# Windowed attention with split values and scaled probabilities, a mask written through DRAM, and gate columns split earlier

## The chip, the cores and the metric

The kernel runs on one core of a Trainium2 chip. The metric is device time in microseconds (us), the median of several runs of the whole program. A core has a matrix engine (PE, with its weight loads shown as PEld), a vector engine (DVE), a scalar engine (ACT), a general engine (POOL) and a queue engine (SP). Each takes its instructions in the order in which they were written for it; DMA queues move data between DRAM and the on-chip memory, and matmul results land in eight banks of accumulator memory (PSUM), of which this kernel uses four for the large products and four for everything else.

## The reference

One decoder block over 512 tokens of width 2048: a modulated RMS norm, one wide input projection, a gated delta-rule branch and a windowed-attention branch, each projected back and merged by gates. The change touches the attention and the two gate columns per head of the delta rule (`b_a`, `a_a`).

```python
beta = jax.nn.sigmoid(b_a.astype(jnp.float32))
g = -jnp.exp(a_log[l]...) * jax.nn.softplus(a_a... + dt_bias[l]...)
...
qb = rms_norm(q_b.reshape(B, T, SWA_HEADS, SWA_HEAD_DIM), q_norm_gain[l])
kb = rms_norm(k_b.reshape(B, T, SWA_KV_HEADS, SWA_HEAD_DIM), k_norm_gain[l])
vb = v_b.reshape(B, T, SWA_KV_HEADS, SWA_HEAD_DIM)
o_b = sliding_window_attention(qb, kb, vb, sinks[l], rel_bias)
y_swa = (o_b * jax.nn.silu(z_b)) @ w_branch_swa[l]

def sliding_window_attention(q, k, v, sinks, rel_bias):
    # 16 query heads of 64, 4 key heads, blocks of 128 queries that see their own and the previous block
    logits = jnp.einsum("bnqhgd,bnkhd->bnhgqk", qb, kb) * (d ** -0.5)
    logits = jnp.where(valid, logits + bias, -jnp.inf)
    m = jnp.maximum(jnp.max(logits, axis=-1, keepdims=True), sink)
    p = jnp.exp(logits - m)
    probs = p / (jnp.sum(p, axis=-1, keepdims=True) + jnp.exp(sink - m))
    out = jnp.einsum("bnhgqk,bnkhd->bnqhgd", probs, vb)
```

## The kernel before

**The frame.** All large products run as three matmuls on split operands: a float32 number is written as `hi` (rounded by a cast on ACT, L184) plus `lo` (the rest, a subtraction on DVE, L185), and hi·hi, hi·lo and lo·hi are added up. The weights are cut into 464 *halves*. `run` (L236) goes through them: for half s it issues the loads of coming weights on SP, the split of half s+2 (`w_cast`, `whi` on ACT and `wlo` on DVE), then one step of each *lane* (a generator that does other work up to its next `yield`), and then the 12 matmuls of half s. One such round is a *tick*; the order is fixed when the program is written, and every engine keeps it. So the matmuls of the next half stand behind whatever the lanes gave PE in that tick, and `whi`/`wlo` of half s+2 stand behind what the lanes gave ACT and DVE in the tick before. Three weight buffers (`wraw`) of two halves each and four buffers each for `whi` and `wlo` are the slack.

**The lanes.** `gdn_all` (L1380) runs the gates of the delta rule (`gdn_gates`), its two groups of four heads (`gdn_group`), then `swa_bias`, then waits for the attention's inputs and runs `swa_attend` and `load_branches`. `keys_lane` runs `swa_keys`. The small results of the lanes lie in four PSUM banks (`side`, L80) that are taken in turn.

**Gate columns.** `gdn_gates` splits 16 columns of the input projection (`wab` into `wabr`) in the first tick after the first stage (`plan_start`, 8 column blocks in five parts, where DVE also does the convolutions) and multiplies them with all of `hhi` and `hlo` in the following four ticks (`ps_ab`).

**Mask.** `swa_bias` builds 16 rows of 384 values (`vec`) and one POOL DMA writes each of them 128 times to DRAM (`vecd`), from where `load` reads a skewed 128x256 mask per head.

**Attention.** `swa_keys` scales the keys, writes hi and lo twice side by side (`kd`) and transposes them on PE (32 transposes) into `kTh`/`kTl`. `Attn` treats four query heads (a group g, four groups) over four blocks n: `prep` scales the queries and splits them (`qhl`), `turn_q` transposes them (16 transposes per group); `logits` makes 8 matmuls and adds the mask (L1055); `soft` takes exponentials on ACT; `turn` transposes the probabilities (`pT`, one bank per key block); `values` multiplies them in full float32 with the values (each such matmul runs as two passes, 64 columns wide) and divides by the sum; `finish` transposes the result back (8 per group) and multiplies with the gate. `swa_attend` runs block i's `logits`, block i-1's `soft`, block i-2's `turn` and block i-3's `values` in an *iteration* of two ticks, and puts the next group's `norm`, `prep`, `load`, `turn_q` between (`todo`).

Of the kernel before, what the change touches and what calls it, by code (L numbers as in the profile page):

```python
# [16 lines left out]
P = 128  # L17
# [20 lines left out]
def tile_hybrid_block(  # L38
# [539 lines left out]
    def gdn_gates():  # L578
# [10 lines left out]
        yield  # L589
# [46 lines left out]
        V.tensor_copy(t1, gh[:, 0:32].bitcast(F32))  # L636
        yield
# [305 lines left out]
    kTh, kTl = [], []  # L943
# [22 lines left out]
    def swa_keys():  # L966
        rsqrt(flat(rs_[:, 16:20]), flat(sq[:, 16:20]), 16, 1.0 / HD, EPS)
        kd_ = [s4("kd", F32R).rearrange("p (t h w d) -> p t h w d", t=2, h=4, w=2) for _ in range(2)]

        def turn_keys(kT_):  # L970
            for h in range(4):
                pt = side("ps_kT")
                for t in range(NT):
                    TE.transpose(pt[:, t * P:(t + 1) * P],
                                 kd_[t // 2][:, t % 2, h].rearrange("p w d -> p (w d)").bitcast(F32), ident)
                if h % 2 == 0:
                    kT_.append(v3(s4("kT", F32R), 2))
                S.copy(kT_[h // 2][:, h % 2], pt)
                if h % 2 == 1:
                    yield  # L980
# [11 lines left out]
        yield from turn_keys(kTh)  # L992
        for t in range(NT):
            for w in range(2):
                kw = kd_[t // 2][:, t % 2, :, w]
                V.tensor_tensor(kw, k3(t), kw.bitcast(F32), op=ALU.subtract)
            yield
        yield
        yield from turn_keys(kTl)
# [3 lines left out]
    class Attn:  # L1003
# [25 lines left out]
        def turn_q(self, i):  # L1029
            if i == 0:  # L1030
                self.qT = []
            self.qT.append(v3(s4("qT", F32R), 2))
            for h in (2 * i, 2 * i + 1):
                pt = side("ps_qT")
                for t in range(NT):
                    TE.transpose(pt[:, t * P:(t + 1) * P],
                                 self.qhl[t // 2][:, t % 2, h].rearrange("p w d -> p (w d)").bitcast(F32), ident)
                S.copy(self.qT[i][:, h % 2], pt)
# [44 lines left out]
        def values(self, n, pT, mx):  # L1083
            g = self.g
            V.tensor_tensor(mx[:, 3], mx[:, 3], mx[:, 4], op=ALU.add)
            V.reciprocal(mx[:, 3], mx[:, 3])
            V.tensor_scalar(mx[:, 3], mx[:, 3], 0.5, None, op0=ALU.mult)
            if n == 0:
                self.osb = s4("osb").rearrange("p (t n) -> p t n", t=NT)
            pv = side("ps_pv")  # L1090
            for h in range(4):
                for kb in pT:
                    t = n - 1 + kb
# [366 lines left out]
```

## Time and profile before

| | |
|---|---|
| median of 3 runs | 1537.3 us (1535.39 to 1538.13) |
| the profiled execution | 1534.27 us, its span 1532.5 us |
| busy: PE, DVE, ACT, POOL | 97%, 54%, 36%, 4% of the span |
| mean granted clock of PE | 0.989 |
| the chain that ended last | PE 89%, DVE 5%, DMA 4% |

How to read it: the span goes from the first to the last instruction. A matmul's listed time is that of one through the pipeline, so consecutive ones overlap; the distance of their starts is what one costs. In a list of groups, "idle before" is time in which the engine waited ahead of that group, with what ended the wait. In a timeline, a wait stands in brackets behind the row. [...]

### The profile page before, as it was taken

Reading aid. Unit: us, or ns where it says so; the run is one execution under the profiler, and the core shown is the slowest. Engines: PE = TensorE matmul, PEld = TensorE weight load, DVE = VectorE, ACT = ScalarE, POOL = GpSimd, SP = SyncE. Lnnn points to the kernel's source line nnn. Section 1 sums busy time; section 2 is a strip of 40 time slices with the busy share of each in tenths; the row PEclk is TensorE's granted clock in tenths of the full one; section 3 lists DMA queues with packets and bytes.
Section 4 is the critical chain, followed back from the end, with each engine's and each line's share of the span. In section 5 each row is a group of like instructions: output and inputs, shape, how many; then the busy total and the mean of one; then the engine's idle time right before and its main releaser. Section 6 shows DMA issues by size and latency. Waiting matters only on the chain.

```text
span 1532.5 us, 19447 instructions
## 1 busy us (share of the span) xinstructions
PE 1484.5 (97%) x7254; PEld 1225.8 (80%) x7254; DVE 827.4 (54%) x1707; ACT 545.4 (36%) x1225; POOL 62.9 (4%) x108
## 2 busy tenths in 40 slices
PE   4989998899999999999989999999999999999998
PEld 1768787688888888888868888888888888888887
DVE  3477886666755446533523566643333766754332
ACT  4522343364323453222423454443332223222221
POOL 0000000111201020200000000000000000000000
PEclk9989999999999999999999999999999999999999
DMA  9697633223422434423573322225545676564432
GB/s 322 237 343 247 198 97 97 69 83 97 138 69 69 154 94 120 126 71 110 125 150 91 115 70 85 81 83 189 155 137 200 212 261 219 180 220 151 149 105 103
DMA packets 161480, 223.16 MB, mean 146 GB/s; under 512 B 14469, under 2 KB 111030, under 8 KB 161386
## 3 DMA queue, kind: packets, MB, share of 16 engines
q1 hardware_dynamic: 152920, 207.87, 42.5%
q0 software_dynamic: 3584, 13.11, 3.8%
q10 hardware_dynamic: 4882, 0.94, 0.3%
q8 instruction: 57, 0.93, 0.3%
q14 instruction: 37, 0.30, 0.1%
HBM read 198.82 MB, written 23.07 MB: 145 GB/s over the span
## 4 chain that ended last, share of the span: by engine, by line
PE 89%; DVE 5%; DMA 4%; ACT 1%; issue 1%; SPq 0%; ACTq 0%; DVEq 0%
PE acc L188 17%; PE acc L190 17%; PE acc L189 17%; PE acct L498 6%; PE acct L499 6%; PE acct L500 6%; PE acc L532 3%; PE acc L533 3%; PE acc L538 3%; DMA wraw<-in_w_in_dram 2%; PE ps_pv L1094 2%; DMA wada<-in_w_ada_dram 1%; DVE kq L394 1%; DVE wlo L185 1%; DVE part L551 1%
## 5 line engine op out<-in xcount | busy, mean ns | idle before, releaser
L185 DVE TENSOR_TENSOR wlo<-wraw,whi 128x512 fp32r<-128x512 f32 x464 | 322.1, 696 | 515.2 <-ACT whi L184 510.3
L184 ACT CAST whi<-wraw 128x512 fp32r<-128x512 f32 x464 | 285.4, 621 | 572.6 <-PE acc L189 298.1
L188 PE MATMUL acc<-hhi,whi 128*128 128x512 f32 x896 | 356.8, 398 | 2.4 <-ACT whi L184 2.4
L190 PE MATMUL acc<-hhi,wlo 128*128 128x512 f32 x896 | 350.1, 391 | 0.7 <-DVE wlo L185 0.5
L189 PE MATMUL acc<-hlo,whi 128*128 128x512 f32 x896 | 349.5, 390 | 0.0
L190 PEld LDWEIGHTS acc<-hhi,wlo 128*128 128x128 f32 x896 | 168.3, 188 | 38.0 <-DVE wlo L185 2.0
L188 PEld LDWEIGHTS acc<-hhi,whi 128*128 128x128 f32 x896 | 168.7, 188 | 35.9 <-ACT whi L184 3.2
L189 PEld LDWEIGHTS acc<-hlo,whi 128*128 128x128 f32 x896 | 168.7, 188 | 32.2
L532 PE MATMUL acc<-hhi,whi 128*128 128x512 f32 x256 | 103.7, 405 | 2.5 <-ACT part L549 1.1
L533 PE MATMUL acc<-hhi,wlo 128*128 128x512 f32 x256 | 101.7, 397 | 0.0
L188 PE MATMUL acc<-oh,whi 128*128 128x512 f32 x256 | 100.9, 394 | 0.0
L498 PE MATMUL acct<-whi,mh 128*128 128x512 f32 x256 | 100.1, 391 | 0.1
L190 PE MATMUL acc<-oh,wlo 128*128 128x512 f32 x256 | 99.6, 389 | 0.0
L500 PE MATMUL acct<-whi,ml 128*128 128x512 f32 x256 | 99.6, 389 | 0.0
L499 PE MATMUL acct<-wlo,mh 128*128 128x512 f32 x256 | 99.6, 389 | 0.0
L189 PE MATMUL acc<-ol,whi 128*128 128x512 f32 x256 | 99.6, 389 | 0.0
L498 PE MATMUL acct<-whi,hhi 128*128 128x512 f32 x192 | 77.1, 401 | 6.3 <-ACT whi L184 6.3
L499 PE MATMUL acct<-wlo,hhi 128*128 128x512 f32 x192 | 75.7, 394 | 0.0
L500 PE MATMUL acct<-whi,hlo 128*128 128x512 f32 x192 | 75.4, 393 | 0.0
L538 PE MATMUL acc<-hlo,whi 128*128 128x512 f32 x256 | 70.2, 397 | 0.0
L532 PEld LDWEIGHTS acc<-hhi,whi 128*128 128x128 f32 x256 | 49.3, 193 | 17.2 <-issue 2.4
L538 PEld LDWEIGHTS acc<-hlo,whi 128*128 128x128 f32 x256 | 49.2, 192 | 10.6
(276 smaller groups left out, 1829.6 us busy)
## 6 DMA issues: line engine op xcount, KB each, us to landing
wraw<-in_w_in_dram SPq DMA_DIRECT2D x168, 512.0 KB, 3.7
wada<-in_w_ada_dram SPq DMA_DIRECT2D x48, 512.0 KB, 7.3
wgate<-in_w_ada_dram SPq DMA_DIRECT2D x32, 512.0 KB, 5.7
wraw<-in_w_out_dram SPq DMA_DIRECT2D x32, 512.0 KB, 4.1
wada<-in_w_ada_dram SPq DMA_DIRECT2D x32, 256.0 KB, 6.6
tgd<-tg SPq DMA_DIRECT2D x16, 512.0 KB, 3.0
wraw<-in_w_branch_gdn_dram SPq DMA_DIRECT2D x16, 512.0 KB, 3.6
wraw<-in_w_branch_swa_dram SPq DMA_DIRECT2D x16, 512.0 KB, 3.5
```

The source lines that it names most:

```text
L184: S.copy(hi, src)
L185: V.tensor_tensor(lo, src, hi.bitcast(F32), op=ALU.subtract)
L188: TE.matmul(o, lhsT=whi, rhs=mhi, start=start, stop=False)
L189: TE.matmul(o, lhsT=whi, rhs=mlo, start=False, stop=False)
L190: TE.matmul(o, lhsT=wlo, rhs=mhi, start=False, stop=stop)
L498: TE.matmul(st["ac"][t], lhsT=sh, rhs=wh, start=(k_ == 0), stop=False)
L499: TE.matmul(st["ac"][t], lhsT=sh, rhs=wl, start=False, stop=False)
L500: TE.matmul(st["ac"][t], lhsT=sl, rhs=wh, start=False, stop=(k_ == KT - 1))
L532: TE.matmul(st[ci][m], lhsT=hi[:, i, ms], rhs=mh_, start=(k == k0), stop=False)
L533: TE.matmul(st[ci][m], lhsT=lo[:, i, ms], rhs=mh_, start=False, stop=False)
L538: TE.matmul(st[ci][m], lhsT=hi[:, i, ms], rhs=ml_, start=False, stop=(k == k0 + nk - 1))
L1094: TE.matmul(pv[:, h * HD:(h + 1) * HD], lhsT=pT[kb][:, h * P:(h + 1) * P], rhs=kvt[t // 2][:, t % 2, 256 + g * HD:256 + (g + 1) * HD], sta ...
```

## The change

Five things are written differently.

- **Gate columns.** The split of `wab` moves out of `gdn_gates` into `gates_prep`, which runs four ticks before the end of the first stage; `ps_ab` now starts in the tick in which the split used to stand, and one more tick lies ahead of `ps_g`.
- **Mask.** `swa_bias` runs between the two groups of heads, and POOL writes the 16 rows to DRAM once (`vec1`) and then copies them 128 times from DRAM to DRAM.
- **Keys and queries.** They are transposed unsplit (two heads per transpose, 8 transposes of keys, 8 of queries per group); hi and lo are made from the transposed tile, 64 partitions at a time.
- **Probabilities and values.** The values are split once (`vhl`, hi and lo side by side); `scale` divides the probabilities by their sum on DVE; `turn` splits the transposed ones (`pTh`, `pTl`); `values` has two matmuls of 512 columns per key block, whose result stands transposed, its hi part in partitions 0 to 63 and its lo part in 64 to 127; ACT copies one and DVE adds the other (`osT`). `finish` has no transposes.
- **Order.** In an iteration, `soft` now stands ahead of `logits` in the first tick; `scale`, `values` and `turn` stand in the second.

```diff
-    def gdn_gates():
+    wabs = []
+
+    def gates_prep():
         nw = KT * 32
...
         S.activation(rows[:, 0:8], rows[:, 0:8], AF.Exp)
-        yield
+        wabs.append(wabr)
+
+    def gdn_gates():
+        wabr = wabs.pop()
         psab = side("ps_ab")
...
         yield
+        yield
         yield
         psg = side("ps_g")
...
     def swa_bias():
...
-        G.dma_start(vecd, vec.unsqueeze(1).broadcast_to([16, P, 384]))
+        G.dma_start(vec1, vec)
+        G.dma_start(vecd, vec1.unsqueeze(1).broadcast_to([16, P, 384]))
         yield
...
-            for w in range(2):
-                S.copy(kd_[t // 2][:, t % 2, :, w], k3(t))
-            yield
...
+            S.copy(vw[:, :, 0], v_)
+            V.tensor_tensor(vw[:, :, 1], v_, vw[:, :, 0].bitcast(F32), op=ALU.subtract)
+            yield
+        yield
+
+        for i in range(2):
+            pt = side("ps_kT")
+            for t in range(NT):
+                TE.transpose(pt[:, t * P:(t + 1) * P], kvt[t // 2][:, t % 2, i * P:(i + 1) * P], ident)
+            kTh.append(v3(s4("kTh", F32R), 2))
+            kTl.append(v3(s4("kTl", F32R), 2))
+            for j in range(2):
+                for w in range(2):
+                    ws = slice(64 * w, 64 * w + 64)
+                    S.copy(kTh[i][ws, j], pt[64 * j:64 * j + 64])
+                    V.tensor_tensor(kTl[i][ws, j], pt[64 * j:64 * j + 64], kTh[i][ws, j].bitcast(F32),
+                                    op=ALU.subtract)
+            yield
...
-                qv = self.qhl[t // 2][:, t % 2]
-                S.copy(qv[:, :, 0], q3)
-                V.tensor_tensor(qv[:, :, 1], q3, qv[:, :, 0].bitcast(F32), op=ALU.subtract)
...
-            for h in (2 * i, 2 * i + 1):
-                pt = side("ps_qT")
-                for t in range(NT):
-                    TE.transpose(pt[:, t * P:(t + 1) * P],
-                                 self.qhl[t // 2][:, t % 2, h].rearrange("p w d -> p (w d)").bitcast(F32), ident)
-                S.copy(self.qT[i][:, h % 2], pt)
+            c0 = (self.g % 2) * 256 + i * P
+            pt = side("ps_qT")
+            for t in range(NT):
+                TE.transpose(pt[:, t * P:(t + 1) * P], qtok[self.g // 2, t // 2][:, t % 2, c0:c0 + P], ident)
+            for j in range(2):
+                src = pt[64 * j:64 * j + 64]
+                S.copy(self.qT[i][0:64, j], src)
+                V.tensor_tensor(self.qT[i][64:128, j], src, self.qT[i][0:64, j].bitcast(F32), op=ALU.subtract)
...
+        def scale(self, n, pe, mx):
+            n0 = 128 if n == 0 else 0
+            V.tensor_tensor(mx[:, 3], mx[:, 3], mx[:, 4], op=ALU.add)
+            V.reciprocal(mx[:, 3], mx[:, 3])
+            for h in range(4):
+                V.tensor_scalar(pe[:, h, n0:], pe[:, h, n0:], mx[:, 3, h:h + 1], None, op0=ALU.mult)
...
-                pT[kb] = s2("pT")
-                if kb:
-                    S.copy(pT[kb], pt)
-                else:
-                    V.tensor_copy(pT[kb], pt)
+                pT[kb] = s2("pTh", F32R), s2("pTl", F32R)
+                split(*pT[kb], pt)
...
-            for h in range(4):
-                for kb in pT:
-                    t = n - 1 + kb
-                    TE.matmul(pv[:, h * HD:(h + 1) * HD], lhsT=pT[kb][:, h * P:(h + 1) * P],
...
+            for kb in pT:
+                t = n - 1 + kb
+                lhsT = vhl[t // 2][:, t % 2, g].rearrange("p w d -> p (w d)")
+                for i in range(2):
+                    TE.matmul(pv, lhsT=lhsT, rhs=pT[kb][i], start=(kb == min(pT) and i == 0), stop=(kb == 1 and i == 1))
+            pv4 = pv.rearrange("p (i j q) -> p i j q", i=2, j=2)
+            for j in range(2):
+                o = self.osT[64 * j:64 * j + 64, :, n * P:(n + 1) * P]
+                S.copy(o, pv4[64:128, :, j])
+                V.tensor_tensor(o, pv4[0:64, :, j], o, op=ALU.add)
...
         def finish(self):
-            ob = obT[self.g]
-            for i in range(2):
-                pt = side("ps_obT")
-                for n in range(NT):
-                    TE.transpose(pt[:, n * P:(n + 1) * P], self.osb[:, n, i * P:(i + 1) * P], ident)
-                V.tensor_tensor(ob[:, i], pt, ob[:, i], op=ALU.mult)
+            V.scalar_tensor_tensor(obT[self.g], self.osT, 0.5, obT[self.g], op0=ALU.mult, op1=ALU.mult)
...
-    run(n_start - LATE)
+    run(n_start - 4 - LATE)
+    gates_prep()
+    run(4)
...
+        yield from swa_bias()
         yield from gdn_group(g1)
-        yield from swa_bias()
```

What this does to the order is shown at three places. The first is DVE at the end of the first stage. Before, the split of the gate columns (`wabr`) stands behind the last partial sums (`part`) and two taps of a convolution (`kq`); `wlo` is the weight split of a coming half:

```order
L1378 SCALAR_TENSOR_TENSOR gkrow<-gkrow,krow_113 128x64
L185 TENSOR_TENSOR wlo_1964<-wraw_1895,whi_1963 128x512
L551 TENSOR_TENSOR part_591<-acc_384_1926,part_591 128x512
L551 TENSOR_TENSOR part_591<-acc_385_1927,part_591 128x512
L394 SCALAR_TENSOR_TENSOR kq_1787<-part_451,cols,kq_1787 128x511
L394 SCALAR_TENSOR_TENSOR kq_1787<-part_451,cols,kq_1787 128x510
L586 TENSOR_TENSOR wabr_1972<-wab_114,wabr_1972 128x16x16
L185 TENSOR_TENSOR wlo_1995<-wraw_1895,whi_1994 128x512
```

After the change the same split stands on DVE four halves earlier, between two taps of an earlier convolution and the next weight split:

```order
L394 SCALAR_TENSOR_TENSOR kq_1650<-part_415,cols,kq_1650 128x509
L407 SCALAR_TENSOR_TENSOR kq_1650<-th_1858,kq_1650 128x512
L588 TENSOR_TENSOR wabr_1873<-wab_114,wabr_1873 128x16x16
L185 TENSOR_TENSOR wlo_1880<-wraw_1806,whi_1879 128x512
L551 TENSOR_TENSOR part_516<-acc_368_1837,part_516 128x512
```

So nothing of the end of the first stage stands ahead of the gate columns on DVE any more.

The second place is DVE in an attention iteration, before: the copy of one transposed block (`pT`), the gate products of a finished group (`zsb`), then the small divisions (`mx`) and one product that divides the values (`osb`):

```order
L185 TENSOR_TENSOR wlo_7788<-wraw_7636,whi_7787 128x512
L414 SCALAR_TENSOR_TENSOR zsb_7791<-th_7792,acc_7419 128x512
L1080 COPY pT_7800<-ps_pT_7795 128x512
L1106 TENSOR_TENSOR zsb_7079<-ps_obT_7814,zsb_7079 128x512
L1106 TENSOR_TENSOR zsb_7079<-ps_obT_7820,zsb_7079 128x512
L185 TENSOR_TENSOR wlo_7844<-wraw_7636,whi_7843 128x512
L414 SCALAR_TENSOR_TENSOR zsb_7791<-th_7847,acc_7420 128x512
L1085 TENSOR_TENSOR mx_7573<-mx_7573 128x4
L1086 RECIPROCAL mx_7573<-mx_7573 128x4
L1087 TENSOR_SCALAR mx_7573<-mx_7573 128x4
L1097 TENSOR_TENSOR osb_7749<-ps_pv_7853,mx_7573 128x256
```

And after, the second tick of an iteration:

```order
L185 TENSOR_TENSOR wlo_7459<-wraw_7264,whi_7458 128x512
L1076 TENSOR_TENSOR mx_7341<-mx_7341 128x4
L1077 RECIPROCAL mx_7341<-mx_7341 128x4
L1079 TENSOR_SCALAR pe_7340<-pe_7340,mx_7341 128x256 x4
L1107 TENSOR_TENSOR osT_7378<-ps_pv_7468,osT_7378 64x2x128 x2
L185 TENSOR_TENSOR pTl_7483<-ps_pT_7477,pTh_7482 128x512
L185 TENSOR_TENSOR pTl_7492<-ps_pT_7486,pTh_7491 128x512
L185 TENSOR_TENSOR wlo_7508<-wraw_7363,whi_7507 128x512
```

Four products on the probabilities, two additions and two subtractions now stand between two weight splits.

The third place is ACT in the same iterations, here with what each row waits for. Before, in a tick with `turn_q`: the weight cast, the copy of a transposed block, the exponentials (`pe`, `mx`), and four casts of transposed queries (`qT`) that wait for PE alone:

```order
L184 CAST whi_7686<-wraw_7543 128x512 [waits DMAHW0_49,PE_49,Activation_49]
L1078 COPY pT_7695<-ps_pT_7690 128x512 [waits PE_49]
L1066 ACTIVATE pe_7572,mx_7573<-pe_7572,mx_7573 128x256 x4
L1068 ACTIVATE mx_7573<-mx_7573 128x4
L1038 CAST qT_7702<-ps_qT_7703 128x512 [waits PE_49]
L1038 CAST qT_7702<-ps_qT_7709 128x512 [waits PE_49]
```

After, in such a tick:

```order
L1106 COPY osT_7378<-ps_pv_7670 64x2x128 [waits PE_49]
L1106 COPY osT_7378<-ps_pv_7670 64x2x128 [waits DVE_49]
L184 CAST pTh_7684<-ps_pT_7679 128x512 [waits PE_49,Activation_49]
L1041 CAST qT_7688<-ps_qT_7689 64x512 [waits PE_49]
L1041 CAST qT_7688<-ps_qT_7689 64x512 [waits DVE_49]
L1041 CAST qT_7698<-ps_qT_7699 64x512 [waits PE_49]
L1041 CAST qT_7698<-ps_qT_7699 64x512 [waits DVE_49]
```

Of each bank, ACT now takes the second half of the partitions only after DVE has finished with the first.

## Rows read from the trace of the kernel before

**Rows 1.** Page, part 1: busy us, share of the span, instructions.

```profile
PE 1484.5 (97%) x7254; PEld 1225.8 (80%) x7254; DVE 827.4 (54%) x1707; ACT 545.4 (36%) x1225; POOL 62.9 (4%) x108
```

**Rows 2.** Groups of instructions: line, engine, names, shapes, count | busy, mean ns | idle.

```profile
L1094 PE MATMUL ps_pv<-kvt,pT 128*128 128x64 f32 x224 | 26.7, 271 | 0.0
```

**Rows 3.** Timeline of PE in one iteration: start us, us, line, names, count.

```profile
905.66 1.89 PE L1094 MATMUL ps_pv<-kvt,pT 128*128 128x64 f32 x16
...
907.36 0.37 PE L1049 MATMUL ps_l<-kT,qT 128*128 128x256 f32 x1
...
908.40 0.40 PE L188 MATMUL acc<-hhi,whi 128*128 128x512 f32 x1
...
910.92 0.40 PE L190 MATMUL acc<-hhi,wlo 128*128 128x512 f32 x1
...
911.15 1.04 PE L1075 MATMUL ps_pT<-cs,pe 128*128 128x128 f32 x8
...
911.95 0.48 PE L188 MATMUL acc<-hhi,whi 128*128 128x512 f32 x1
```

**Rows 4.** Windows in the attention: stretch, its us, busy us (count), PEclk, DMA share, GB/s.

```profile
900.00:920.00 20.00, 20.00 (x121) 17.66 (x120) 14.31 (x59) 9.28 (x28) 0.00 (x0) 1.00 0.29 83
920.00:940.00 20.00, 20.00 (x129) 17.81 (x128) 12.48 (x49) 10.21 (x32) 0.00 (x0) 1.00 0.16 50
940.00:960.00 20.00, 20.00 (x125) 17.76 (x124) 14.79 (x57) 9.59 (x31) 0.00 (x0) 1.00 0.42 132
960.00:980.00 20.00, 20.00 (x127) 17.82 (x126) 12.12 (x43) 11.52 (x37) 0.00 (x0) 1.00 0.10 27
```

**Rows 5.** Groups of instructions on DVE, ACT and POOL that resemble the added ones.

```profile
L1097 DVE TENSOR_TENSOR osb<-ps_pv,mx 128x256 f32<-128x256 f32 x16 | 6.8, 425 | 4.6 <-PE ps_pv L1094 3.4
L1257 DVE TENSOR_SCALAR ga<-wgate,cc 128x512 f32<-128x512 f32 x4 | 1.9, 481 | 0.0
L1341 DVE TENSOR_SCALAR x<-x,xr 128x1024 f32<-128x1024 f32 x8 | 5.4, 749 | 0.0
L1080 DVE COPY pT<-ps_pT 128x512 f32<-128x512 f32 x12 | 8.3, 688 | 10.5 <-PE ps_pT L1075 10.5
L1038 ACT CAST qT<-ps_qT 128x512 fp32r<-128x512 f32 x16 | 8.2, 585 | 3.9 <-PE ps_qT L1036 3.9
L834 ACT COPY la<-ps_z 64x256 f32<-64x256 f32 x8 | 2.5, 364 | 4.0 <-PE ps_z L831 4.0
L660 POOL TENSOR_TENSOR ug<-cs,gv 128x512 fp32r<-128x512 f32 x16 | 19.1, 1214 | 344.3 <-DVE gv L636 289.1 <-PE ps_o L885 44.7 <-issue 10.5
```

**Rows 6.** DMA issues: names, queue, count, KB each, median us to landing.

```profile
vecd<-vec POOLq DMA_DIRECT2D x1, 3072.0 KB, 34.6
...
XN<-scr POOLq DMA_DIRECT2D x8, 64.0 KB, 3.2
```

**Rows 7.** Windows while the mask is written: columns as in rows 4.

```profile
780.00:785.00 5.00, 0.00 (x0) 0.00 (x0) 0.00 (x0) 0.00 (x0) 0.00 (x0) 0.81 0.99 135
```

**Rows 8.** Timeline of ACT and PE there: start us, us, row, [idle before <-releaser].

```profile
785.17 0.62 ACT L184 CAST whi<-wraw 128x512 fp32r<-128x512 f32 x1 [14.41 <-DMA wraw<-in_w_in_dram]
...
779.15 0.39 PE L500 MATMUL acct<-whi,hlo 128*128 128x512 f32 x1
785.84 0.80 PE L498 MATMUL acct<-whi,hhi 128*128 128x512 f32 x1 [6.30 <-ACT whi L184]
...
790.05 0.39 PE L498 MATMUL acct<-whi,hhi 128*128 128x512 f32 x1
```

**Rows 9.** Timeline of PE at the end of the first stage.

```profile
248.12 0.39 PE L190 MATMUL acc<-hhi,wlo 128*128 128x512 f32 x1
252.63 0.77 PE L594 MATMUL ps_ab<-hhi,wabr 128*128 128x512 f32 x1 [4.12 <-DVE wabr L586]
...
257.46 0.39 PE L188 MATMUL acc<-hhi,whi 128*128 128x512 f32 x1
```

**Rows 10.** Windows behind that: columns as in rows 4.

```profile
260.00:270.00 10.00, 10.00 (x45) 8.20 (x44) 2.66 (x5) 2.44 (x5) 0.00 (x0) 1.00 0.33 107
...
280.00:290.00 10.00, 8.61 (x41) 6.97 (x40) 8.12 (x30) 2.04 (x4) 0.38 (x1) 1.00 0.11 38
290.00:300.00 10.00, 8.95 (x38) 6.60 (x36) 8.41 (x11) 3.62 (x7) 4.60 (x4) 1.00 0.18 52
```

**Rows 11.** Timeline of PE there.

```profile
289.06 0.83 PE L641 MATMUL ps_g<-gv,cs 128*128 128x32 f32 x6 [1.39 <-DVE gv L631]
```

## What the change does to the time: the prediction

> **What bounds the kernel now.** I read the busy line first: PE is busy 97% of the span, DVE 54%, ACT 36% [rows 1]. Then four windows of the attention: PE 20.00 of 20 us in each, DVE 14.31, 12.48, 14.79 and 12.12 [rows 4], so there each microsecond taken off PE counts, until another engine is late. Last the three places where PE does stand: ahead of the gate columns [rows 9], behind them [rows 10, 11], and while the mask is written [rows 7, 8]. All sums below are made against the profiled execution, 1534.3 us; the median, 1537.3, is 3.0 above it, and I add the sum to that.
>
> **Unit prices on PE.** A main matmul costs the distance of two starts: (910.92 − 908.40) / 11 = 0.229 us, a half of twelve 2.75. A value pass: 16 from 905.66 to 907.36, 0.106. Eight logits from 907.36 to 908.40: 0.13. Eight transposes from 911.15 to 911.95: 0.10 [rows 3].
>
> **Values.** 224 passes [rows 2] × 0.106 = 23.8 us go. In their place: a group has four blocks of queries with two key blocks each, less the one that the first block lacks, so 7 × 4 groups × 2 (hi, lo) = 56 matmuls of 512 columns, × 0.229 = 12.8. Gain 11.0.
>
> **Transposes.** Keys go from 32 to 8, queries from 64 to 32, outputs from 32 to none: 88 × 0.10 = 8.8 us, of which the keys are 2.4 (on PE ahead of the attention) and the attention 6.4. So PE gets 11.0 + 6.4 = 17.4 us lighter within the attention and 2.4 ahead of it.
>
> **Gate columns.** PE starts its last product at 248.12 and `ps_ab` only at 252.63: less 0.229 for the product, 4.28 us of standing. Behind it the products start slowly: from 252.63 to 257.46 are 4.83 us for eleven intervals, where 11 × 0.229 is 2.52; 2.31 more [rows 9]. With the split done four halves earlier both go: 6.6 us. The split itself costs DVE and ACT the same work at another place, some 0.42 us on DVE (by the product of 256 columns, 425 ns) [rows 5]; there it can delay a `wlo` by no more than this, and two halves of split weights lie ahead of PE: 0, at most 0.4. Is the gain given back behind it? From 260 to 270 PE is busy 10.00 and DVE 2.66, so the time is kept there; from 280 to 300 DVE is busy 16.5 of 20 and PE 17.6 [rows 10], so DVE and its hand-offs bound that stretch as much as PE. But the work of that stretch starts when PE has made its products, and these are all 6.6 us earlier. The extra tick ahead of `ps_g` lets the chain of small DVE steps end before PE needs it; the 1.39 us that PE waits there [rows 11] may go, or turn up as the wait behind it: 0, range −1.4 to 0.
>
> **Mask.** From 780 to 785 PE does nothing, and the DMA engines are busy 0.99 [rows 7]: the 3072 KB broadcast takes 34.6 us [rows 6], and a weight load stands behind it. ACT waits 14.41 us for `wraw`, PE from 779.15 to 785.84: less 0.229, 6.46 us. The next twelve intervals take 785.84 to 790.05 = 4.21 instead of 2.75: 1.46 more [rows 8]. Together 7.9. The change moves the broadcast ahead of the second group of heads and takes its source from DRAM. No row shows a copy from DRAM to DRAM. Its ends: the same engines for the same 34.6 us and the same stall (gain 0, what rival C says), or no stall (7.9). I take 7.9 by the rows nearest: three weight buffers of two halves are 6 × 2.75 = 16.5 us of cover, the broadcast of before ran that cover out only by 6.5, and DRAM as source asks nothing of the 16 partitions that all packets of before came from.
> [...]
> What is queued behind the moved step: POOL must wait for `vec1` to land (3.2 us for a 64 KB write [rows 6]) before it issues the copy, and behind these stand two `ug` products of 1.21 us [rows 5] for the second group of heads. With two issues at about 1 us (not shown; the same order as a POOL instruction), 3.2 + 2.0 + 2.4 = 7.6 us against three halves, 8.25 us, until PE wants them: 0, at most 3.
>
> **Keys' turn.** In each of two ticks ACT and DVE alternate over one bank: four casts at 0.585 and four subtractions at about 0.69 [rows 5] = 5.1 us at full width, against a half of 2.75 plus 0.4 of transposes. The weight splits behind them are two halves ahead: 0, at most 1.
>
> **DVE in the attention.** This is where I expect part of the gain to go back. A group is four iterations, 8 halves. PE before: 22.0 (halves) + 4.2 (32 logits) + 2.8 (28 transposes of probabilities) + 5.9 (56 passes) + 1.6 + 0.8 (queries, outputs) = 37.3 us. After: 22.0 + 4.2 + 2.8 + 3.2 (14 matmuls) + 0.8 = 33.0. DVE before: 53.7 of 80 us [rows 4], so 24.8 per group. Added:
> - scales of the probabilities: 12 of 256 columns and 4 of 128. The nearest rows are TENSOR_SCALAR of 512 columns, 481 ns, and of 1024, 749 [rows 5]; the line through them gives 0.35 and 0.28: 5.3 us.
> - sums of the two halves: 8 of 256 columns in place of 4 products: +4 × 0.425 = 1.7.
> - subtractions for `pTl`: 7 in place of 3 copies of 0.69: 2.8.
> - queries: four subtractions from PSUM (0.69) in place of four from SBUF (0.425): 1.1. `finish`: 0.
>
> That is 10.9. Hand-offs come on top, in which DVE stands: ACT takes the second half of the partitions of a bank only after DVE has finished with the first, so DVE waits a copy of 0.364 [rows 5] and some 0.17 around it, four times per group for `osT`; for the second subtraction of a query bank it waits a cast of 0.585, twice: 2.1 + 1.2 = 3.3 us. 24.8 + 10.9 + 3.3 = 39; consecutive instructions on DVE overlap by about 0.1 us, so 37 to 39, and I take 38: 5.0 above PE's 33.0. It binds where all of it comes together, in the second and third group; in the first there are no values and no `finish` yet, in the last no `prep`. So 2 × 5.0 = 10 us are given back, and PE's idle time there should be this.
> [...]
>
> **The sum.** −17.4 (attention on PE) − 2.4 (keys) − 6.6 (gates) − 7.9 (mask) + 10 (DVE) = −24.3. 1534.3 − 24.3 = 1510.0 for such an execution, **1513** as median.
>
> **Rivals.**
> - *DVE hides under PE* (1503). If neither hand-offs nor scales hold PE up, the 10 us stay: 1537.3 − 34.3. For it: the weight splits run two halves ahead, and the sum of instructions alone, 24.8 + 10.9 − 1.3 = 34.4, is hardly above 33. Against it: those hand-offs.
> - *The broadcast stalls at its new place too* (1521). By 3072 KB in 34.6 us at 0.99 of the DMA engines [rows 6, 7]: 1513 + 7.9. The engines' share of 0.99 speaks for it, since they may be full whatever the source.
> - *The gates' gain is given back* from 280 on (1520): DVE at 16.5 of 20 [rows 10] would have to be late by all of 6.6; I see no row that says so.
> - *Slower: a serial chain in every iteration* (1546). All small results share four banks taken in turn. If PE's next bank comes free only after the sums, their hand-offs and one subtraction have drained, PE stands for 2 × 0.425 + 2 × (0.364 + 0.17) + 0.69 = 2.6 us in each iteration: 33.0 / 4 + 2.6 = 10.9 against 37.3 / 4 = 9.3 before. That is 1.6 × 16 = 26 slower, less the 16.9 of keys, gates and mask: 1537.3 + 26 − 16.9 = 1546. It decides from 16.9 / 16 = 1.1 us per iteration above before, 2.1 us of standing. Against it: a half's 2.75 us of products lies between one use of a bank and the next but one.
>
> **How the numbers follow.** Forecast 0.48; DVE hidden 0.22; broadcast stalls 0.17; gates given back 0.07; serial chain 0.06. Forecast and first rival span 1503 to 1513, the broadcast reaches 1521; with the bounds of DVE's price (37 to 39 per group: ±2; POOL and keys +4; `ps_g` −1.4) the range is **1502 to 1526**, which leaves out the serial chain and what lies beyond these bounds. About 0.2%, 3.1 us, is what a measurement tells from no change. Faster 0.91, within 0.04, slower 0.05: slower is the serial chain; within is its lighter form.
>
> **What would show it.** In the profile of the changed kernel: `ps_pv` has 56 matmuls and PE's time on it falls to some 12.8; no idle ahead of `ps_ab` near 248; no idle of PE and full clock while the mask is copied, and little ahead of `ug` behind it; PE idle ahead of logits, transposes or weights in the second and third group, about 5 us each, ended by DVE, and DVE busy 90% or more there. If DVE is at 80% and PE at 100% there, the first rival holds. If PE stands where `vecd` is written, the second does. If PE stands ahead of every `ps_pv` or `ps_l` for a microsecond, the last does.

## The result and the profile after

Measured once more on another occasion it took 1510.6 against 1535.4: 0.9835 (0.9820 to 0.9850). The forecast was 1513, the range 1502 to 1526.

The first line of the page of the changed kernel (busy us, share of the span, instructions), against [rows 1]:

```profile
PE 1461.7 (97%) x6998; PEld 1200.1 (80%) x6998; DVE 862.4 (57%) x1787; ACT 557.2 (37%) x1249; POOL 63.6 (4%) x109
```

PE has 22.8 us less to do and DVE 35.0 us more. To see where the time went, I follow two products of PE that stand in both kernels: the first of the last small products on the first stage's input side (`ps_mod`), and the first one that uses the attention's result (`oh`). In the timeline of PE (start us, us, row), before:

```profile
194.78 0.91 PE L364 MATMUL ps_mod<-one,accv 128*128 128x1 f32 x7
...
1174.91 0.39 PE L188 MATMUL acc<-oh,whi 128*128 128x512 f32 x1
```

and after:

```profile
195.77 0.61 PE L364 MATMUL ps_mod<-one,accv 128*128 128x1 f32 x5
...
1152.00 0.39 PE L188 MATMUL acc<-oh,whi 128*128 128x512 f32 x1
```

Between the two lies all that the change touches. The changed kernel comes to the first 0.99 us later and to the second 22.91 us earlier: 23.90 us gained in the stretch. In the 195 us ahead of it, where both kernels do the same, the profiled executions of this study differ: they start the stretch between 0.11 us earlier and 4.73 us later than that of before. The medians hold such differences too, so below each kernel is given by what it gains in the stretch as well; the two executions of the changed kernel give 23.90 and 23.93.

### The profile page after: what moved, and what is told of

It reads as the page before. It is cut to its first block, busy times and chain, and to the rows that moved or that the text cites. A ratio compares the mean times of both kernels' runs of the same rounds, so it can differ in the third digit from the quotient of the medians.

```text
span 1509.3 us, 19073 instructions
## 1 busy us (share of the span) xinstructions
PE 1461.7 (97%) x6998; PEld 1200.1 (80%) x6998; DVE 862.4 (57%) x1787; ACT 557.2 (37%) x1249; POOL 63.6 (4%) x109
## 4 chain that ended last, share of the span: by engine, by line
PE 87%; DVE 8%; DMA 2%; ACT 2%; issue 1%; SPq 0%; ACTq 0%; DVEq 0%
PE acc L188 16%; PE acc L190 16%; PE acc L189 15%; PE acct L499 7%; PE acct L498 7%; PE acct L500 7%; PE acc L532 4%; PE acc L533 4%; PE acc L538 4%; DMA wada<-in_w_ada_dram 1%; DVE wlo L185 1%; PE ps_kk L721 1%; DVE pe L1059 1%; DVE pe L1079 1%; PE ps_row L337 1%
```

## The parts, one at a time

Gain in the stretch, from the starts of the same two products in each trace (the first shift taken from the second), and the ratio to the kernel before:

| kernel | shift at 195 | shift at 1175 | in the stretch | ratio (95%) |
|---|---|---|---|---|
| changed | +0.99 | −22.91 | −23.90 | 0.9818 (0.9801–0.9835) |
| changed, again | +1.36 | −22.57 | −23.93 | 0.9835 (0.9820–0.9850) |
| gate columns alone | +2.60 | −5.29 | −7.89 | 0.9956 (0.9939–0.9973) |
| mask alone | −0.11 | −8.85 | −8.74 | 0.9938 (0.9923–0.9953) |
| mask, DRAM row at the old place | +2.91 | −5.87 | −8.78 | 0.9944 (0.9928–0.9959) |
| mask, on-chip rows at the new place | +4.73 | +11.88 | +7.15 | 1.0042 (1.0026–1.0059) |
| attention and keys alone | +0.10 | −2.50 | −2.60 | 0.9994 (0.9983–1.0005) |
| attention, keys and mask | +3.70 | −11.57 | −15.27 | 0.9908 (0.9894–0.9923) |

**Gate columns alone** (`gates_only`): the kernel before with this.

```diff
-    run(n_start - LATE)
+    run(n_start - 4 - LATE)
+    gates_prep()
+    run(4)
...
         V.tensor_copy(t1, gh[:, 0:32].bitcast(F32))
+        yield
         yield
         yield
         psg = side("ps_g")
```

> The kernel before with the gate columns' split moved into the first stage and the extra tick ahead of ps_g, nothing else. By the prediction's term, -6.6 us: 4.28 of waiting and 2.31 of slow products ahead and at ps_ab, nothing behind. By the trace of the changed kernel, -9: there PE's lead over before grew from 6.6 at ps_ab to 9.0 behind ps_g, so the wait of 1.39 us at ps_g and about 1.0 of waits behind it would go too. If the gain is given back to DVE from 280 us on: -3 to 0. Bounds between the three: -7.8 and -4.8.

It gains 7.89 us in the stretch, and had gained 8.89 by 523 us. 1.0 of that goes again at the mask: PE waits 6.56 us there instead of 6.30, and more of its products behind the wait fall into the time at a lower clock (the granted clock PEclk, as a share of full speed, is 0.50 and 0.86 in the 10 us from 779, against 0.51 and 1.00 from 785 before). In the changed kernel, whose mask holds nobody up, the gates are worth 23.90 − 15.27 = 8.6. So the wait at `ps_g` went too, and 0.7 us of the waits behind it (0.97, 0.50 and 1.40 us before, 0.27, 0.43 and 1.44 after). In the changed kernel's timeline of PE these two rows have no wait (which would stand in brackets), against 4.12 in [rows 9] and 1.39 in [rows 11]:

```profile
246.58 0.39 PE L599 MATMUL ps_ab<-hhi,wabr 128*128 128x512 f32 x1
...
281.85 0.75 PE L647 MATMUL ps_g<-gv,cs 128*128 128x32 f32 x6
```

**Mask alone** (`mask_only`), and its two halves: the same place with the old source (`mask_sbuf`), the new source at the old place (`mask_oldplace`).

```diff
-        G.dma_start(vecd, vec.unsqueeze(1).broadcast_to([16, P, 384]))
+        G.dma_start(vec1, vec)
+        G.dma_start(vecd, vec1.unsqueeze(1).broadcast_to([16, P, 384]))
...
+        yield from swa_bias()
         yield from gdn_group(g1)
-        yield from swa_bias()
```

`mask_only` has both pieces, `mask_oldplace` the first, `mask_sbuf` the second.

> The kernel before with the mask built between the two groups of heads and copied from a DRAM row, nothing else. No stall at the new place: -7.9 us, the copy lands in about 15 us (15.1 in the changed kernel), PE has no wait while it runs. If POOL's wait for the row holds up the second group of heads: up to +3 of that back, seen as PE waiting for ug. If the copy fills the DMA engines as before: 0, with a wait of ACT for wraw near 540 us.

> The kernel before with the mask built between the two groups of heads but written from the 16 on-chip rows as before, no DRAM row. If the source sets the duration (16 partitions), it lands after about 34.6 us here too, the weights wait as before, PE stands for some 6 us and the time moves by no more than 1.5 us. If the place alone brought the gain (the loads of the second group's stage leave room), -7.9 with no wait of ACT for wraw.

> The kernel before with the mask copied from a DRAM row, but built behind the second group of heads as before. If the source sets how long the copy takes, it lands in about 15 us (15.1 in the changed kernel), the weights wait less than their buffers cover, and PE's wait of 6.30 us with the slow products behind goes here too: -7.9 to -8.7 us from 195 us to the end. If the place matters as well: a wait of ACT for wraw of 5 us or more near 770 and 2 to 5 us of PE's wait stay.

The source alone brings the gain: −8.78 at the old place, −8.74 at the new. The place alone costs: +7.15, where I expected no more than 1.5 either way. The DMA issues (KB, us to landing) of the changed kernel

```profile
vecd<-vec POOLq DMA_DIRECT2D x1, 3072.0 KB, 15.1
```

of the on-chip rows at the new place

```profile
vecd<-vec POOLq DMA_DIRECT2D x1, 3072.0 KB, 36.9
```

and of the DRAM row at the old place

```profile
vecd<-vec POOLq DMA_DIRECT2D x1, 3072.0 KB, 15.4
```

say why: the same 3072 KB in 15 us from the rows in DRAM, 35 to 37 from 16 partitions ([rows 6] 34.6). 15 us is inside the 16.5 us that three weight buffers cover by the prediction's estimate, 35 is not, at either place. With the old source at the new place ACT waits 19.51 us for weights, and PE stands for 13.33, about twice the 6 us that I expected:

```profile
573.45 0.62 ACT L184 CAST whi<-wraw 128x512 fp32r<-128x512 f32 x1 [19.51 <-DMA wraw<-in_w_in_dram]
...
575.68 1.19 PE L667 MATMUL ps_dec<-ug,alr 128*128 128x512 f32 x2 [13.33 <-ACT junkp L685]
```

The listed releaser of PE is an ACT row that stands behind that late cast, so the weights are the cause. From 570 to 580 PE's granted clock is 0.50, and the products behind the wait are slow too (0.43 us from start to start from 576.67 on, instead of 0.229). Why the wait is longer here than at the old place no run takes apart. 3072 KB are 91 GB/s in 34.6 us and 208 GB/s in 15.1; what makes the on-chip source the slower one, the runs do not show.

**Attention and keys alone** (`attn_only`): the kernel before with the new `swa_keys`, `Attn` and `swa_attend`.

```diff
-                pT[kb] = s2("pT")
...
+                pT[kb] = s2("pTh", F32R), s2("pTl", F32R)
+                split(*pT[kb], pt)
```

> The kernel before with the attention, keys and queries of the changed one and their order, and the gates and the mask as before. By the prediction's terms -17.4 -2.4 +10 = -9.8 us. By the trace of the changed kernel PE waits 10.9 us in the attention and loses some 1.7 more where its clock falls to 0.91, so -17.4 -2.4 +12.6 = -7.2. If DVE did not bind: -19.8. The three single parts should add to the whole change (-28.8 by medians, -23.2 by the profiled executions).

This missed: 2.60 us where I expected 7 to 10, and by the medians nothing; the three single parts, which I expected to add up, come to 19.2 of 23.9. PE's waits in the attention were as in the changed kernel (10.6 us in all); the loss lies ahead of them. In the timelines of PE and ACT:

```profile
785.70 0.80 PE L498 MATMUL acct<-whi,hhi 128*128 128x512 f32 x1 [7.55 <-ACT whi L184]
...
796.40 0.51 PE L498 MATMUL acct<-whi,hhi 128*128 128x512 f32 x1 [1.80 <-ACT whi L184]
```

```profile
785.03 0.62 ACT L184 CAST whi<-wraw 128x512 fp32r<-128x512 f32 x1 [18.07 <-DMA wraw<-in_w_in_dram]
...
787.00 0.58 ACT L993 CAST kTh<-ps_kT 64x512 fp32r<-64x512 f32 x1 [0.87 <-DVE kTl L994]
...
795.73 2.18 ACT L184 CAST whi<-wraw 128x512 fp32r<-128x512 f32 x4
```

Two things happen. In [rows 8] PE went on at 785.84. It does less for the keys now, and only stands longer, 7.55 instead of 6.30 us, till the same broadcast has ended: what is gained while everybody waits for one transfer is lost. Then it waits again, 2.75 us in four waits up to 797 (0.33, 0.31, 1.80 and 0.31). ACT's copies of the keys (`kTh`), which take turns with DVE, stand behind the late weight cast and ahead of the next ones, until 795.73. The prediction put this alternation at 0, at most 1, because the weight splits run two halves ahead; behind the broadcast that lead is used up. 1.25 and 2.75 make 4.0. My theory of then had only the first. The test of this is attention and mask together, without the gates (`attn_mask`):

> Attention, keys and order of the changed kernel and its mask, but the gate columns as before. Theory: the attention alone moved the time so little because the mask's broadcast at the old place ends when it ends (PE went on at 785.84 before and 785.70 with the attention alone), so the keys' 2.4 us and more were eaten there. Then, with the mask moved, the parts add: -8.65 (mask alone) -2.4 (keys) -3.9 (attention in the changed kernel) = -15 us from 195 us to the end. If the attention part is worth less for another reason: -10 to -11.

It gains 15.27, the −15 of this theory, and PE has no wait between 740 and 850 in it, so the second loss is gone with the first. Attention and keys are worth 15.27 − 8.74 = 6.5 once the mask is out of the way, 3.9 more than alone. The whole is 8.6 + 8.7 + 6.5 = 23.9, which as a chain of differences adds up by itself.

## What holds PE up in the attention

The forecast had PE's work 17.4 us lighter there and 10 us of it given back, because DVE is late. PE's waits of the changed kernel (engine, line waited for: us in total, times, longest), of which the kernel before has none:

```profile
PE ps_l L1053 <- DVE osT L1107: 6.6, 5, 2.5
...
PE ps_pT L1086 <- DVE mx L1059: 3.6, 3, 1.4
...
PE ps_pT L1086 <- DVE qT L1042: 0.6, 2, 0.3
```

10.8 us in all, every one released by DVE. Five windows (columns as in [rows 4]) show DVE at 83 to 90% and PE short of 20 in each:

```profile
880.00:900.00 20.00, 17.81 (x95) 14.91 (x95) 17.29 (x57) 14.27 (x46) 0.00 (x0) 1.00 0.26 80
900.00:920.00 20.00, 19.72 (x103) 16.19 (x101) 16.66 (x60) 9.44 (x25) 0.00 (x0) 1.00 0.19 53
920.00:940.00 20.00, 15.87 (x84) 13.21 (x84) 17.97 (x64) 13.13 (x43) 0.00 (x0) 1.00 0.34 106
940.00:960.00 20.00, 19.07 (x101) 15.40 (x99) 16.75 (x54) 10.33 (x27) 0.00 (x0) 1.00 0.19 53
960.00:980.00 20.00, 16.54 (x78) 13.82 (x79) 17.08 (x61) 11.68 (x39) 0.00 (x0) 0.91 0.25 80
```

The waits aren't spread over the groups. They stand at the three changes of group, where the two query turns, two blocks of probabilities and, at the second and third, soon after `finish` meet: 2.2 us at the first, 4.3 at the second and third. PE at the second:

```profile
920.45 0.63 PE L1086 MATMUL ps_pT<-cs,pe 128*128 128x128 f32 x4 [0.28 <-DVE qT L1042]
922.47 0.66 PE L1086 MATMUL ps_pT<-cs,pe 128*128 128x128 f32 x4 [1.39 <-DVE mx L1059]
...
928.81 0.36 PE L1053 MATMUL ps_l<-kTh,qT 128*128 128x256 f32 x1 [2.46 <-DVE osT L1107]
```

PE waits for a side bank that an earlier result still holds: the logits, which DVE reads at L1059, the queries (L1042), or the values, which DVE adds at L1107. Why is DVE late? Its timeline there, and ACT's:

```profile
925.35 0.68 DVE L414 SCALAR_TENSOR_TENSOR zsb<-th,acc 128x512 f32<-128x512 f32 x1
925.95 0.15 DVE L1076 TENSOR_TENSOR mx<-mx 128x4 f32<-128x4 f32 x1
926.14 0.18 DVE L1077 RECIPROCAL mx<-mx 128x4 f32<-128x4 f32 x1
926.35 1.14 DVE L1079 TENSOR_SCALAR pe<-pe,mx 128x256 f32<-128x256 f32 x4
927.41 0.41 DVE L1107 TENSOR_TENSOR osT<-ps_pv,osT 64x256 f32<-64x256 f32 x1
928.25 0.42 DVE L1107 TENSOR_TENSOR osT<-ps_pv,osT 64x256 f32<-64x256 f32 x1 [0.43 <-ACT osT L1106]
```

```profile
927.85 0.37 ACT L1106 COPY osT<-ps_pv 64x256 f32<-64x256 f32 x1 [3.69 <-DVE osT L1107]
```

DVE works without a gap until the second addition, and stands 0.43 us there for a copy that ACT could have made 3.69 us earlier, had it not been put behind DVE's first addition. At 928.67 the bank is free, and at 928.81 PE goes on. Three edits of the changed kernel tell apart work, hand-offs and the burst in one tick.

**Copies first** (`copies_first`), for the values and in the same way for the queries:

```diff
             for j in range(2):
-                o = self.osT[64 * j:64 * j + 64, :, n * P:(n + 1) * P]
-                S.copy(o, pv4[64:128, :, j])
-                V.tensor_tensor(o, pv4[0:64, :, j], o, op=ALU.add)
+                S.copy(oj[j], pv4[64:128, :, j])
+            for j in range(2):
+                V.tensor_tensor(oj[j], pv4[0:64, :, j], oj[j], op=ALU.add)
```

> The changed kernel, but ACT issues both copies of a value bank (and of a query bank) before DVE's two operations, so that ACT's second copy no longer waits for DVE's first. If DVE's standing in these hand-offs is part of what binds (theory: DVE is late by work plus hand-offs): DVE loses its 0.43 us wait in each iteration and two of 0.65 in each change of group, some 2.2 us in each of the three stretches in which PE waits, so PE's waits in the attention fall from 10.9 to 4 to 6 us and with them most of the 1.7 us at a lower clock: -5 to -8 us. If the order of the four side banks alone holds PE up: no change. If the copies, now earlier, delay ACT's weight casts: a new wait of PE for whi, up to +2.

**Scales on POOL** (`pool_scale`):

```diff
-                V.tensor_scalar(pe[:, h, n0:], pe[:, h, n0:], mx[:, 3, h:h + 1], None, op0=ALU.mult)
+                G.tensor_scalar(pe[:, h, n0:], pe[:, h, n0:], mx[:, 3, h:h + 1], None, op0=ALU.mult)
```

> The changed kernel with the four products that scale the probabilities on POOL instead of DVE. DVE then has 1.15 us less in each iteration (four overlapped products, 912.97 to 914.12 in the trace), 2.3 in each of the three stretches in which PE waits; if DVE's time binds there: PE's waits fall from 10.9 to about 4, -5 to -8 us. If POOL needs more than 8 us for an iteration's four products, PE waits for pe from POOL instead, up to +2 per iteration, +30. If POOL's work makes DVE's instructions longer (mean of wlo above 0.70), part of the gain goes. If the order of the banks alone holds PE up: no change.

**Query turns in two ticks** (`spread`):

```diff
-                         a_.load, lambda a_=a_: a_.turn_q(0), lambda a_=a_: a_.turn_q(1)])
+                         lambda a_=a_: a_.turn_q(0), a_.load, lambda a_=a_: a_.turn_q(1)])
```

> The changed kernel with one of the two query turns one tick earlier (it changes places with the load of the mask), all work the same. If the burst counts (values, two blocks of probabilities and two query banks in one tick, five side banks where there are four), PE's waits for mx and qT ahead of the transposes, 4.2 us of the 10.9, go: -3 to -5 us. If DVE's total time over the iteration binds, the wait only moves to the next logits: within 1 us.

And together: all three (`cf_pool_spread`), or the first two (`cf_pool`).

> All three edits on the changed kernel: copies first, scales on POOL, query turns in two ticks. If DVE's time and hand-offs bind, DVE has 2 us to spare in each iteration and PE's waits in the attention are under 1 us, the clock stays at 1.00 there: -11 to -13 us against the changed kernel. If something else holds PE up (the order of the banks, ACT), 4 us or more of waiting stay.

> Copies first and scales on POOL, the query turns in one tick as in the changed kernel. If DVE's time with its hand-offs is all that bound: PE's waits in the attention under 1.5 us, within 1.5 us of the version with all three edits. If the burst of five side banks in one tick costs something by itself: 2 us or more of PE waiting for mx or osT stay.

| kernel | shift at 195 | shift at 1175 | in the stretch | against changed | median us, ratio (95%) |
|---|---|---|---|---|---|
| copies first | +2.39 | −28.11 | −30.50 | −6.6 | 1505.1, 0.9799 (0.9772–0.9826) |
| scales on POOL | +0.75 | −34.65 | −35.40 | −11.5 | 1499.6, 0.9768 (0.9744–0.9792) |
| query turns in two ticks | +1.69 | −21.86 | −23.55 | +0.35 | 1511.0, 0.9840 (0.9811–0.9869) |
| all three | +2.13 | −36.73 | −38.86 | −15.0 | 1496.7, 0.9749 (0.9723–0.9775) |
| first two | +1.80 | −37.20 | −39.00 | −15.1 | 1496.5, 0.9740 (0.9723–0.9756) |

PE's waits in the attention, with the copies first

```profile
PE ps_l L1054 <- DVE osT L1109: 4.8, 3, 2.0
```

with the scales on POOL

```profile
PE ps_l L1053 <- DVE osT L1107: 2.5, 2, 1.3
...
PE ps_pT L1086 <- DVE mx L1059: 0.4, 2, 0.2
```

and with the query turns in two ticks

```profile
PE ps_l L1053 <- DVE osT L1107: 6.3, 3, 2.5
...
PE ps_qT L1038 <- DVE qtok L1023: 1.8, 2, 1.1
...
PE ps_pT L1086 <- DVE mx L1059: 1.6, 3, 0.6
```

The spread of the burst only moves the waits (9.7 us are left): it isn't the number of banks taken in one tick. Less work on DVE, or less standing, takes them away: it is DVE's time around the change of group. Copies first came out as expected in the waits and in the gain; the time at the lower clock did not go with them, it stands behind 928 instead (0.91 in the window from 920 to 940). The scales on POOL gave 11.5 us, more than the 5 to 8 that I expected: 7.9 us of waits went, and the time at the lower clock, 1.6 us, too (all windows from 860 to 1000 stand at 1.00); the other 2.0 lie in the rows about the waits. All three gave 15.0 where I expected 11 to 13: such rows, which I had not counted, are in that too. With the first two edits PE waits for nothing in the attention any more, the burst left as it was:

```profile
880.00:900.00 20.00, 20.00 (x109) 17.17 (x109) 16.79 (x59) 13.26 (x43) 8.59 (x9) 1.00 0.27 80
900.00:920.00 20.00, 20.00 (x111) 17.20 (x110) 18.52 (x57) 15.01 (x41) 5.97 (x8) 1.00 0.19 54
920.00:940.00 20.00, 20.00 (x108) 17.06 (x107) 17.79 (x65) 11.90 (x40) 10.40 (x12) 1.00 0.43 132
940.00:960.00 20.00, 20.00 (x111) 17.11 (x110) 18.00 (x58) 13.59 (x38) 8.41 (x9) 1.00 0.26 79
960.00:980.00 20.00, 20.00 (x107) 17.10 (x106) 14.58 (x46) 12.93 (x43) 9.31 (x12) 1.00 0.21 59
```

DVE may be busy 18.5 of 20 us and PE still never wait. This kernel beats the changed one by 14.1 us on the same occasion (1496.5 against 1510.6):

> The changed kernel itself, to stand on the same chip beside the others: from 195 us to the end -23.9 us against the first profiled execution of before, within 0.5 us, whatever the first 195 us do; PE's waits in the attention 10.9 us, within 0.5.

The repetition gave 23.93 in the stretch and the same waits (6.7, 3.6 and 0.6 us).

More of the change, by code (lines that the diff above doesn't have):

```diff
@@ L928, in tile_hybrid_block @@
     vecd = dp.tile([16, P, 384], F32, name="vecd")
+    vec1 = dp.tile([16, 384], F32, name="vec1")
     def swa_bias():
@@ L942, in tile_hybrid_block @@
     rs_ = kp.tile([P, 20, NT], F32, name="rs_")
-    kTh, kTl = [], []
+    kTh, kTl, vhl = [], [], []
     def plan_swa(ch):
@@ L967, in swa_keys @@
         rsqrt(flat(rs_[:, 16:20]), flat(sq[:, 16:20]), 16, 1.0 / HD, EPS)
-        kd_ = [s4("kd", F32R).rearrange("p (t h w d) -> p t h w d", t=2, h=4, w=2) for _ in range(2)]
-        def turn_keys(kT_):
-            for h in range(4):
-                pt = side("ps_kT")
-                for t in range(NT):
-                    TE.transpose(pt[:, t * P:(t + 1) * P],
[L975 to L979, printed above, removed]
-                    yield
         def k3(t):
@@ L987, in swa_keys @@
             V.tensor_tensor(k3(t), k3(t), gkrow.unsqueeze(1).broadcast_to([P, KVH, HD]), op=ALU.mult)
-            for w in range(2):
-                S.copy(kd_[t // 2][:, t % 2, :, w], k3(t))
+            if t % 2 == 0:
+                vhl.append(s4("vhl", F32R).rearrange("p (t h w d) -> p t h w d", t=2, h=4, w=2))
+            v_ = kvt[t // 2][:, t % 2, 256:512].rearrange("p (h d) -> p h d", d=HD)
+            vw = vhl[t // 2][:, t % 2]
+            S.copy(vw[:, :, 0], v_)
+            V.tensor_tensor(vw[:, :, 1], v_, vw[:, :, 0].bitcast(F32), op=ALU.subtract)
             yield
         yield
[L992 to L996, printed above, removed]
+        for i in range(2):
[10 more added lines that the diff above has]
+                                    op=ALU.subtract)
             yield
-        yield
-        yield from turn_keys(kTl)
     obT = []
@@ L1011, in norm @@
             rsqrt(flat(rs_[:, 4 * g:4 * g + 4]), flat(sq[:, 4 * g:4 * g + 4]), 16, 1.0 / HD, EPS)
-            self.qhl = [s4("qhl", F32R).rearrange("p (t h w d) -> p t h w d", t=2, h=4, w=2) for _ in range(2)]
         def prep(self, ts):
@@ L1075, in turn, with values @@
                     TE.transpose(pt[:, h * P:(h + 1) * P], pe[:, h, kb * P:(kb + 1) * P], ident)
-                pT[kb] = s2("pT")
-                if kb:
-                    S.copy(pT[kb], pt)
-                else:
-                    V.tensor_copy(pT[kb], pt)
+                pT[kb] = s2("pTh", F32R), s2("pTl", F32R)
+                split(*pT[kb], pt)
             return pT
-        def values(self, n, pT, mx):
+        def values(self, n, pT):
             g = self.g
-            V.tensor_tensor(mx[:, 3], mx[:, 3], mx[:, 4], op=ALU.add)
-            V.reciprocal(mx[:, 3], mx[:, 3])
-            V.tensor_scalar(mx[:, 3], mx[:, 3], 0.5, None, op0=ALU.mult)
@@ L1088, in values @@
             if n == 0:
-                self.osb = s4("osb").rearrange("p (t n) -> p t n", t=NT)
+                self.osT = v3(s4("osT"), 2)
             pv = side("ps_pv")
-            for h in range(4):
-                for kb in pT:
-                    t = n - 1 + kb
-                    TE.matmul(pv[:, h * HD:(h + 1) * HD], lhsT=pT[kb][:, h * P:(h + 1) * P],
-                              rhs=kvt[t // 2][:, t % 2, 256 + g * HD:256 + (g + 1) * HD],
-                              start=(kb == min(pT)), stop=(kb == 1))
@@ L1124, in swa_attend @@
         for i in range(NI + 3):
-            if 0 <= i - 3 < NI:
-                g, n = divmod(i - 3, 4)
-                heads[g].values(n, st[i - 3, "pT"], st[i - 3, "pe"][1])
-                if n == 3:
-                    todo += [heads[g].finish, heads[g].store]
+            if 0 <= i - 1 < NI:
+                g, n = divmod(i - 1, 4)
+                heads[g].soft(n, *st[i - 1, "pe"])
             if i < NI:
@@ L1133, in swa_attend @@
                 st[i, "pe"] = heads[g].logits(n)
-                if n == 0 and g < 3:
+                if n == 1 and g < 3:
                     todo += prep[g + 1]
+            if todo:
+                todo.pop(0)()
             yield
+            if 0 <= i - 1 < NI:
+                g, n = divmod(i - 1, 4)
+                heads[g].scale(n, *st[i - 1, "pe"])
+            if 0 <= i - 3 < NI:
+                g, n = divmod(i - 3, 4)
+                heads[g].values(n, st[i - 3, "pT"])
+                if n == 3:
+                    todo += [heads[g].finish, heads[g].store]
             if 0 <= i - 2 < NI:
```

7 lines of the change are left out of this document (removed).

## The prediction, point by point

- **PE's work in the attention**, forecast −17.4. In the kernel with the first two edits, in which nothing waits there, PE needs 19.0 us less than before: it is 20.0 us ahead at the product that stands at 815 before, and 39.0 at the end of the stretch. By the distances between starts, values went from 23.6 to 12.8, queries from 6.6 to 3.1, outputs from 3.2 to none, and 1.5 less went to logits, probabilities and main products, which I had not counted. Right, 1.6 too small. The 56 value products are there:

```profile
L1102 PE MATMUL ps_pv<-pTl,vhl 128*128 128x512 f32 x28 | 11.0, 392 | 0.0
L1102 PE MATMUL ps_pv<-pTh,vhl 128*128 128x512 f32 x28 | 10.9, 390 | 0.0
```

- **Gates**, −6.6: measured −8.9 by 523 us, alone as in the changed kernel (8.6 of it are left at the end). The step that was mis-sized is the one on the wait behind (0, range −1.4 to 0): the 1.39 us at `ps_g` and 0.7 us after it went and did not turn up again. The rival that the gain is given back is out.
- **Mask**, −7.9: measured −8.7, and for the reason that was weighed, the source. That POOL's wait costs nothing held: PE waits for `ug` nowhere in this trace (in the changed kernel the row lands in 2.2 us and the two issues list 0.51 and 1.04, where I had 3.2 and about 1 each). The place, which I took as part of the gain, brings nothing. The rival of a stall at the new place (1521) would have come true with the old source, and worse: +7.15 where it had 0. **Keys**: −2.4, and 0 for their turn; both held in the changed kernel, the second only because the mask is out of the way.
- **DVE in the attention**, +10: measured 15.1, the difference of the changed kernel and that with the first two edits (39.00 − 23.90). The mechanism held, by its releaser and its cure; its size did not, and its place only in part. First, I took an average over a group, 38 us of DVE against 33 of PE, in two groups of four (the 24.8 in it should be 25.0: 53.7 of 80 us, of 37.3). In the trace DVE falls behind at each of three changes of group and catches up between them, so that windows of 20 us show it at 83 to 90% and hardly at the "90% or more" that I had named as a sign. The waits at the ends of the second and the third group, where I had expected some 5 us each, come to 4.3 each; the end of the first, which I had left out, costs 2.2. Second, I had no term for PE's clock. After 2.46 us of waiting at 967 the granted clock falls for part of the next windows (0.85 and 0.80), and twelve products take 4.34 us (967.90 to 972.24) instead of 2.75; after a wait of the same 2.46 us at 929 it stays at 1.00 (925 to 935):

```profile
965.00:970.00 5.00, 2.65 (x11) 2.24 (x12) 4.38 (x16) 3.59 (x11) 0.00 (x0) 0.85 0.47 147
970.00:975.00 5.00, 5.00 (x24) 4.11 (x23) 3.50 (x14) 2.07 (x7) 0.00 (x0) 0.80 0.38 108
```

  10.8 us of waits and 1.6 of clock are 12.4; the remaining 2.7 lie in the rows around the waits (a block of four transposes at 0.66 instead of 0.60 and the like), which I can't take apart further.
- **Prices on DVE.** A scale lists 349 ns, as the line through [rows 5] had it (0.35); four of them overlapped take 1.15, 0.28 each. An addition of two halves lists 415 (425 taken), a subtraction for the queries 690 (0.69). What DVE stands for in the hand-offs was under-estimated: 14.5 us ahead of 32 additions and 8.1 ahead of 16 query subtractions, 5.7 per group where I had 3.3 (its 0.17 us around a copy was an estimate of mine that no row shows; at 928 it is 0.06, 0.43 of standing for a copy of 0.37):

```profile
L1107 DVE TENSOR_TENSOR osT<-ps_pv,osT 64x256 f32<-64x256 f32 x32 | 13.3, 415 | 14.5 <-ACT osT L1106 14.5
...
L1042 DVE TENSOR_TENSOR qT<-ps_qT,qT 64x512 fp32r<-64x512 f32 x16 | 11.0, 690 | 8.1 <-ACT qT L1041 7.9
```

- **Rivals.** DVE hidden under PE (1503) is out, by 10.8 us of waits. The serial chain in every iteration (1546) is out: between the changes of group PE doesn't wait.
- **The sum**: forecast −17.4 − 2.4 − 6.6 − 7.9 + 10 = −24.3, measured −23.9 in the stretch. Two more products of PE, before

```profile
770.10 0.39 PE L498 MATMUL acct<-whi,hhi 128*128 128x512 f32 x1
...
814.99 0.39 PE L498 MATMUL acct<-whi,hhi 128*128 128x512 f32 x1
```

and after

```profile
762.15 0.39 PE L498 MATMUL acct<-whi,hhi 128*128 128x512 f32 x1
...
796.00 0.39 PE L498 MATMUL acct<-whi,hhi 128*128 128x512 f32 x1
```

  show where it came from: with the 0.99 us of the start, the changed kernel is 8.9 us ahead at the first (gates), 20.0 at the second (11.0 more by mask and keys) and 23.9 at the end (3.9 more by the attention, 19.0 less 15.1). The total came out this close by luck, because errors cancelled: the gates, the mask and PE's work were 4.7 us better (2.3, 0.8 and 1.6), DVE 5.1 worse. The medians moved by 28.8 and 24.8; what they have over 23.9 no trace shows.

## What to carry to other kernels

Parts that are measured alone need not add up: a transfer that everybody waits for swallows what is gained while it runs (here 7.55 us of waiting instead of 6.30), and when it has used up the slack, work that was hidden shows (2.75 us). So clear that first, then measure the rest. A second engine's average load says little on whether it holds the first one up (DVE at 18.5 of 20 us cost nothing in one kernel, at 16.7 to 18.0 it cost 10.8 us of waits in another); look for the tick in which its jobs pile up, and there for hand-offs in which two engines take turns on one buffer, which a mere change of order (all copies, then all additions; 6.6 us here) can take away. An idle engine, even a slow one (POOL at 0.96 us for a scale of DVE's 0.35), is a good place for a step that is due only an iteration later (11.5 us here).

## What the runs showed of the hardware that I had not expected

- The copy from the rows in DRAM lands in 14.1 to 16.0 us, from 16 partitions in 34.4 to 36.9, for the same bytes. Yet the DMA engines are listed as busy 0.99 at 135 GB/s in [rows 7], and 1.01 and 1.04 at 340 and 325 GB/s in the changed kernel from 525 to 535: a busy share does not say that the transfer couldn't be faster.
- POOL scales a 128x256 tile in 0.96 us (listed mean) and four in 3.6 to 4.2:

```profile
L1080 POOL TENSOR_SCALAR pe<-pe,mx 128x256 f32<-128x256 f32 x48 | 45.4, 964 | 48.1 <-DVE mx L1078 24.3 <-PE ps_pT L1087 9.1 <-ACT pe L1071 7.6
```

  An iteration's 8.25 us hide this. In the kernel with the first two edits, eight `wlo` of DVE that start while POOL is at it list 0.71 us in the mean (one 0.88, the others 0.68 to 0.70), 35 others there 0.69: almost no price on DVE. It shows on POOL: the four products of 128x256 that start as a `wlo` has just begun (0.02 us ahead to 0.16 behind) list 1.31 to 1.43 us, the other 44 list 0.92 to 0.94:

```profile
888.25 0.68 DVE L185 TENSOR_TENSOR wlo<-wraw,whi 128x512 fp32r<-128x512 f32 x1
...
888.29 1.43 POOL L1080 TENSOR_SCALAR pe<-pe,mx 128x256 f32<-128x256 f32 x1
```

  Why POOL's product is longer then, the runs do not show.
